# Order of the work between attention and MLP in a one-layer encoder kernel: operand blocks regrouped, residual rows emitted a row later, bias masks stored later

## The chip, the cores and the metric

The kernel runs on one core of a Trainium2 chip. The metric is the device time of one execution in microseconds; each version is run several times and the median counts. Engines are named as in the profile: PE (TensorE, the matrix engine), PEld (its weight loads), DVE (VectorE), ACT (ScalarE), POOL (GpSimd), SP (SyncE, which issues most DMAs; its queue appears as SPq).

## The reference

One layer of an encoder on 2048 tokens of 1024 features, in float32. Two kinds of attention share one input projection and one output projection; a squared-ReLU MLP follows. Each half has its own RMS norm, with shift, scale and gate from a conditioning vector.

```
mod = silu(c) @ w_ada + b_ada            # sh1, sc1, gt1, sh2, sc2, gt2
h = rmsnorm(x, g1) * (1 + sc1) + sh1
q_sb, k_sb, v_sb, q_ca, k_ca, v_ca = split(h @ w_in)
o_sb = stick_breaking_attention(q_sb, k_sb, v_sb)               # 8 heads
o_ca = chunked_relpos_attention(rms(q_ca), rms(k_ca), v_ca, rel_bias)   # 8 heads
x = x + gt1 * (concat(o_sb, o_ca) @ w_o)
h = rmsnorm(x, g2) * (1 + sc2) + sh2
x = x + gt2 * (relu(h @ w1) ** 2 @ w2)
```

## The kernel before, in words

The work is transposed: features lie on the 128 partitions and 512 tokens form a block `tb` (four of them, also numbered `g`). A float32 operand of PE is kept as a high and a low part (type float32r): ACT casts the high part, DVE subtracts it from the value and so makes the low part, and `mm3` multiplies in three matmuls, high by high, high by low and low by high. Eight such triples, 24 matmuls of 128x512, make one output tile (a row) of a projection; a row is here a tile of 128 features by 512 tokens.

The stages in order of time, from the trace:

- 0 to 440 us: the input projection. The queue `behind` carries small jobs that are run some half jobs later than they are put in. `prepare_wo` splits a slice of the output projection's weights (`wo` into `woh` and `wol`) and stores it to `scr_wo`; `prepare_bias` loads a head's bias window `b`, lets POOL write the mask value into two corners, and stores it to `scr_b`. In both, what follows the load is put in with `behind.add(2, rest)`.
- 440 to 1385: both attentions, with other work mixed in as fillers.
- 1385 to 1474: the turn. PE runs the last rows of the output projection. Four rows `po` of token block 1 come from a filler; `row()` advances that filler to its next row. Then eight `Mixed` rows `pso` of token block 0, as the first eight steps of a list `steps`; three of them find their weights in memory (`resident`, tiles `ow`), and five load `wo` tiles of 1 MB from `scr_wo`. In `Mixed.run` the row's `then()` issues the load of the row three further on, and `residual` follows: DVE multiplies the row by its gate and adds it to the old x (tile `xr`, or `cxr` for a `Mixed` row), and SP stores it to `scr_x`. While PE works on the rows, `right_blocks(1, k, ...)` builds the MLP's first operands for token blocks 2 and 3, in four blocks k = 0 to 3: `load` brings four tiles `cy` from `scr_x`, `scale` multiplies each on POOL by the norm and on ACT by the scale with shift, and seven times `put` makes an operand `h{i}_{k}`, for four of them after a difference of two tiles on DVE.
- 1474 to 1760: `First`, seven products for each pair of hidden slices in the manner of Strassen (`ps<-h,opw`; the weights `w` come in pairs, POOL makes their sums `ts`, and ACT and DVE split them into `opw`; `cu`, `cv` and others hold partial results).
- 1760 to about 2100: `Second` for the same half (`ps<-oph,opv`), and in it the second turn: `norm2`, and `right_blocks(0, k, temp)` for token blocks 0 and 1, each of whose nine jobs is hung on a step with `at(n, job)`. Then `First` and `Second` for that half, up to 2714.

No scheduler orders anything: the wrapper `Ordered` keeps each engine's instructions in the order in which the Python code emits them, and SP issues its DMAs in that order too. So an instruction that waits holds everything behind it on its engine. `later.add(n, job)` runs a job n ticks later, and each step ends with one tick. `kept` takes a tile from a pool of 12 buffers (names beginning with c in the trace, like `cy`, `cxr`, `cu`), `temp` one from a pool of 7 (names beginning with t, like `ty`, `ts`). Eight DMAs of SP may be on their way at a time; the ninth waits for the first.

The order of the turn before is written out at the end of the function, as calls of `row()`, `some(k, ...)` (jobs of block k by their number: 0 load, 1 scale, 2 to 8 the seven puts) and `at`.

Of the kernel before, what the change touches and what calls it, by code (L numbers as in the profile page):

```python
# [9 lines left out]
F32 = mybir.dt.float32  # L10
F32R = mybir.dt.float32r
BF16 = mybir.dt.bfloat16
AF = mybir.ActivationFunctionType
ALU = mybir.AluOpType
# [4 lines left out]
P = 128  # L19
# [6 lines left out]
TB = 512  # L26
# [53 lines left out]
def encoder_kernel(ctx, tc, xT, c, g1, g2, w_in, gqk, bias, w_o, w1, w2, w_ada, b_ada, out):  # L80
    nc = tc.nc
    act, dve, pool, sp = nc.scalar, nc.vector, nc.gpsimd, nc.sync
# [61 lines left out]
    later = Later()  # L144

    def split(hi, lo, src, lo_eng=None):
        act.copy(hi, src)
        (lo_eng or dve).tensor_tensor(lo, src, hi.bitcast(F32), op=ALU.subtract)
# [53 lines left out]
    def mm3(ps, st_hi, st_lo, mv_hi, mv_lo, first, last, more=False):  # L202

        pe.matmul(ps, st_hi, mv_hi, start=first, stop=False, skip_group_check=more)
        pe.matmul(ps, st_hi, mv_lo, start=False, stop=False, skip_group_check=more)
        pe.matmul(ps, st_lo, mv_hi, start=False, stop=last, skip_group_check=more)
# [21 lines left out]
    def residual(g, n, ps, xr):  # L228
        dve.scalar_tensor_tensor(xr, ps, mod[:, 2 * KT + n : 2 * KT + n + 1], xr, op0=ALU.mult, op1=ALU.add)
        stores[0].dma_start(scr_x[g, n], xr)  # L230
# [11 lines left out]
    if True:  # L242
# [20 lines left out]
        behind = Later()  # L263
# [117 lines left out]
        def prepare_bias(h):  # L381
            b = stp.tile([P, WIN], F32, tag="bg", name=f"b{h}", bufs=2)
            sp.dma_start(b, bias[h])

            def rest():
                pool.memset(b[0:HD, WIN - HD :], NEG)
                pool.memset(b[HD:P, 0:HD], NEG)
                sp.dma_start(scr_b[h,], b)

            behind.add(2, rest)  # L390

        xts, hts, ws = {}, {}, {}

# [36 lines left out]
        act, dve, pool = (Ordered(tc, e) for e in (act, dve, pool))  # L430
# [75 lines left out]
        act, dve, pool = nc.scalar, nc.vector, nc.gpsimd  # L506
# [21 lines left out]
        for i in range(NH):  # L528
            todo.insert(6 * i + 2, (1.8, lambda i=i: prepare_bias(i)))
            todo.insert(6 * i + 5, (4.4, lambda i=i: prepare_wo(i)))  # L530
# [62 lines left out]
    if True:  # L593
# [391 lines left out]
        rest = 0  # L985
# [24 lines left out]
        def force(f):  # L1010

            got = next(f.gen, None)
            if callable(got):
                got()
            return None if got is None else callable(got)
# [25 lines left out]
        op = ph.enter_context(tc.tile_pool(name="op", bufs=2))  # L1041
# [54 lines left out]
    HK = KT // 2  # L1096
# [5 lines left out]
    if True:  # L1102
# [4 lines left out]
        hop = {k: pm.enter_context(tc.tile_pool(name=f"hop{k}", bufs=1, side="right")) for k in range(2)}  # L1107
# [3 lines left out]
        def operand(src, nm, eng=None, dst=None):  # L1111

            o = opp.tile([P, 2, TB], F32R, tag="op", name=f"op{nm}") if dst is None else dst
            split(o[:, 0, :], o[:, 1, :], src, eng)
            return o
# [8 lines left out]
        def column_sum(eng, out, a, b, op):  # L1124
            eng.tensor_tensor(out, a, b, op=op)
            return out
# [7 lines left out]
        def bank(nm):  # L1134
            return pp.tile([P, TB], F32, tag="ps", name=f"ps{nm}")
# [3 lines left out]
        def at(n, job):  # L1139
            jobs.setdefault(n, []).append(job)  # L1140


        hops = {}
# [33 lines left out]
        def right_blocks(mb, k, home):  # L1177

            y = {}
            tiles = [(nm, 2 * mb + tb, k + HK * kk) for nm, tb, kk in (("11", 1, 0), ("12", 0, 0), ("21", 1, 1), ("22", 0, 1))]  # L1180

            def load():
                for nm, tb, kk in tiles:
                    y[nm] = home(f"y{mb}_{k}_{nm}")
                    sp.dma_start(y[nm], scr_x[tb, kk])

            def scale():
                for nm, tb, kk in tiles:
                    pool.tensor_tensor(y[nm], y[nm], rows[tb], op=ALU.mult)
                    act.activation(  # L1190
                        y[nm], y[nm], AF.Identity, scale=aff[:, 1, kk : kk + 1], bias=mod[:, 3 * KT + kk : 3 * KT + kk + 1]
                    )

            def put(i, nm, a=None, b=None):

                if a:
                    column_sum(dve, y[nm], y[a], y[b], ALU.subtract)
                hops[i, k] = hop[k].tile([P, 2, TB], F32R, tag=f"h{i}_{k}", name=f"h{mb}_{i}_{k}")
                operand(y[nm], "", dst=hops[i, k])

            puts = ((1, "11"), (5, "11", "12", "11"), (3, "22"), (7, "12", "22", "12"))
            puts += ((6, "22", "22", "11"), (2, "21"), (4, "21", "21", "22"))
            return [load, scale] + [lambda x=x: put(*x) for x in puts]


        class Step:
# [5 lines left out]
            def run(self):  # L1212
                pass
# [100 lines left out]
        def second_sums(j, step):  # L1314

            t = []

            def load():
                t.append(raw_pair([P, 2, 2, TB], F32, f"w2s_{j}"))
                for s in range(2):  # L1320
                    sp.dma_start(t[0][:, s].rearrange("p r n -> p (r n)"), w2[2 * j + s])

            def out(i, dst, a, b, op):
                tile = {nm: t[0][:, s, r, :] for nm, s, r in (("11", 0, 0), ("21", 0, 1), ("12", 1, 0), ("22", 1, 1))}
                column_sum(dve, tile[dst], tile[a], tile[b], op)
                sp.dma_start(scr_s[i - 1 if i < 7 else 0, j // 2][:, j % 2, :], tile[dst])

            at(step - (6 if j else 0), load)
            sums = ((5, "22", "21", "22", ALU.add), (7, "21", "11", "21", ALU.subtract))
            sums += ((6, "11", "22", "11", ALU.subtract), (3, "12", "12", "11", ALU.subtract))  # L1330
            for n, x in enumerate(sums):
                at(step + n + (0 if j else 4), lambda x=x: out(*x))
# [81 lines left out]
        class Mixed(Step):  # L1414
# [26 lines left out]
            def run(self):  # L1441
                g, n = self.g, self.n
                w = self.w
                ps = bank(f"o{g}_{n}")
                for k in range(KT):
                    m = Mixed.parts[k]
                    mm3(ps, w[:, 0, k, :], w[:, 1, k, :], m[:, 0, :], m[:, 1, :], k == 0, k == KT - 1)

                self.then()
                residual(g, n, ps, self.xr)  # L1450


        LEFT = 3
# [5 lines left out]
        for mb in (1, 0):  # L1459
            begin = len(steps)  # L1460
            steps += [First(mb, j, i) for j in range(NP) for i in PRODUCTS]
            for j in range(NP):
                f = steps[begin + 7 * j]
                if mb:
                    second_sums(j, begin + 7 * j + 2)
                if j > mb:
                    at(begin + max(7 * j - 13, 2 if mb else -6), f.load)
                    at(begin + 7 * j - 9, f.fetch)
            if not mb:
                at(begin - 8, steps[begin].load)  # L1470
            if mb:
                end = len(steps)
                norm2(1, end - 8)
                norm2(0, end)
                for k in range(HK):
                    begins = end + 16 + 10 * k
                    for n, job in zip((0, 4, 5, 6, 7, 8, 9, 10, 11), right_blocks(0, k, temp)):
                        at(begins + n, job)
            steps += [Second(mb, i, j) for i in PRODUCTS for j in range(NP)]
            for n in range(begin + 7 * NP, len(steps), 2):  # L1480
                at(n - 7, steps[n].load)


        blocks = [right_blocks(1, k, kept) for k in range(HK)]

        def some(k, *ns):
            for n in ns:
                blocks[k][n]()

        left = filler.pop(0)  # L1490

        def row():
            while force(left) is False:
                pass

        steps[0].fetch(0, KT - 2)
        some(0, 0)
        row()
        row()
        some(0, 1, 2, 3, 4)  # L1500
        row()
        some(1, 0)
        some(0, 5, 6, 7, 8)
        steps[0].fetch(KT - 2, KT)
        row()
        some(1, 1, 2, 3, 4)
        row()
        some(2, 0)
        some(1, 5, 6, 7, 8)
        while force(left) is not None:  # L1510
            pass
        hx.close()
# [2 lines left out]
            del resident[n]  # L1515
        for m in range(LEFT):
            steps[m].load()
        for n, (k, *ns) in enumerate(((2, 1, 2, 3, 4), (2, 5, 6, 7, 8), (3, 1, 2, 3, 4), (3, 5, 6, 7, 8))):
            at(n, lambda k=k, ns=ns: some(k, *ns))
        at(0, lambda: some(3, 0))  # L1520
        ready, used = KT, 0
        ahead = iter(steps[1:])
        nxt = next(ahead)
# [57 lines left out]
```

## Time and profile before

| what | before |
| --- | --- |
| runs | 2721.05, 2716.10, 2713.18 us |
| median | 2716.1 us |
| profiled execution | 2715.61 us, its span 2713.8 us |
| mean granted clock of PE | 0.990 |
| busy share of the span | PE 97%, PEld 82%, DVE 69%, ACT 56%, POOL 39% |
| DMA | 650 MB moved, 240 GB/s on average |

The span runs from the first to the last instruction of the core. A row of the timeline gives the start, the length, the engine, the line, the operation, the tile written and the tiles read, a count of instructions in a row, and in brackets the idle time before them with what ended it. Tiles go by names without their numbers. Nearly all instructions have line 42, as the wrapper records them there, so groups are told apart by tiles. A row of a window gives its bounds and length, the busy time of PE, PEld, DVE, ACT and POOL with the number of instructions, the granted clock, the share of the DMA engines and GB/s. A row of the waits view gives who waits for whose tile: the total, the count and the longest.

### The profile page before, as it was taken

What the parts mean: (1) busy time and instruction counts of PE and PEld (TensorE: products, weight loads), DVE (VectorE), ACT (ScalarE), POOL (GpSimd) and SP (SyncE); (2) the same over time, 40 slices, a digit from 0 to 9 for tenths busy, and PEclk for the clock granted to TensorE, in tenths of its full rate; (3) what the DMA queues carried; (4) which work ended last, traced back from release to release, by engine and by line L of the source; (5) the groups of instructions that cost most, each with busy time, mean ns of one, the idle gap of its engine ahead of it and who ended that gap; (6) DMA issues with size and microseconds to landing.
All of it is one profiled execution on the core that took longest, in us unless ns stands there. A gap on an engine that the chain in (4) does not pass through costs nothing. (4 is left out here: it accounts for less than half of the span.)

```text
span 2713.8 us, 42707 instructions
## 1 busy us (share of the span) xinstructions
PE 2622.7 (97%) x14192; PEld 2233.5 (82%) x14192; DVE 1885.1 (69%) x3159; ACT 1518.2 (56%) x2926; POOL 1063.4 (39%) x1296
## 2 busy tenths in 40 slices
PE   6999999899999999999998999999999999999999
PEld 5899998778878987778876888878788888888887
DVE  6435555788789878989755777768866565655565
ACT  5423444788688878878643454455644454444443
POOL 5464265576467656767533333202001323200000
PEclk9999999999999999999998999999999999999999
DMA  9869977978888687756766776795675444465574
GB/s 344 314 247 346 355 290 215 270 248 260 264 258 245 210 259 251 231 186 214 213 228 242 244 270 251 265 334 202 233 259 177 157 144 160 151 233 194 202 264 155
DMA packets 265579, 650.36 MB, mean 240 GB/s; under 512 B 29200, under 2 KB 65040, under 8 KB 255632
## 3 DMA queue, kind: packets, MB, share of 16 engines
q1 hardware_dynamic: 264576, 645.55, 69.7%
q10 hardware_dynamic: 784, 2.10, 0.3%
q8 instruction: 112, 1.84, 0.3%
q14 instruction: 107, 0.88, 0.1%
HBM read 456.16 MB, written 191.37 MB: 239 GB/s over the span
## 5 line engine op out<-in xcount | busy, mean ns | idle before, releaser
L42 PE MATMUL ps<-oph,opv 128*128 128x512 f32 x2688 | 613.6, 390 | 4.7 <-ACT opv L42 2.7
L42 PE MATMUL ps<-h,opw 128*128 128x512 f32 x2664 | 606.4, 390 | 3.7 <-ACT cu L42 3.2
L42 PEld LDWEIGHTS ps<-oph,opv 128*128 128x128 f32 x2688 | 504.0, 188 | 112.4 <-ACT opv L42 4.0
L42 PEld LDWEIGHTS ps<-h,opw 128*128 128x128 f32 x2664 | 501.1, 188 | 108.7 <-ACT cu L42 3.6
L42 POOL TENSOR_TENSOR b<-b,p 128x512 f32<-128x512 f32 (+1 forms) x320 | 360.2, 1126 | 189.0 <-DVE p L42 166.6
L42 DVE TENSOR_TENSOR wtl<-wt,wth 128x512 fp32r<-128x512 f32 (+3 forms) x544 | 290.5, 545 | 49.6 <-ACT wth L42 47.0
L42 ACT CAST wth<-wt 128x512 fp32r<-128x512 f32 (+3 forms) x544 | 257.8, 485 | 115.2 <-PE wt L42 99.3
L42 PE MATMUL pt<-wh,ht 128*128 128x256 f32 x1664 | 305.7, 285 | 0.9 <-DVE qh L42 0.9
L42 DVE TENSOR_TENSOR oph<-hw,oph 128x512 fp32r<-128x512 f32 x224 | 159.9, 714 | 207.1 <-ACT oph L42 206.9
L42 ACT CAST oph<-hw 128x512 fp32r<-128x512 f32 x224 | 139.2, 622 | 277.4 <-PE ps L42 259.3
L42 DVE TENSOR_TENSOR_SCAN p<-z,p,zero 128x512 f32<-128x512 f32 x192 | 246.0, 1281 | 33.2 <-ACT z L42 28.5
L42 PEld LDWEIGHTS pt<-wh,ht 128*128 128x128 f32 x1664 | 262.0, 193 | 1.2 <-ACT st L42 1.1
L42 POOL TENSOR_TENSOR ts<-w 128x512 f32<-128x512 f32 x32 | 44.5, 1392 | 554.6 <-DMA w<-in_w_dram 511.7
L42 PE MATMUL pt<-wl,ht 128*128 128x256 f32 x832 | 236.3, 284 | 3.0 <-POOL wl L42 3.0
L42 PE MATMUL acc<-wth,v 128*128 128x512 f32 (+3 forms) x544 | 222.6, 413 | 0.5 <-DMA v<-scr_v 0.5
L42 ACT ACTIVATE b<-z 128x512 f32<-128x512 f32 (+1 forms) x320 | 171.7, 537 | 64.9 <-PE z L42 47.2
L42 POOL TENSOR_TENSOR e<-e,cols 128x640 f32<-128x640 f32 (+4 forms) x128 | 143.2, 1122 | 144.3 <-DVE cols L42 82.4
L42 PE MATMUL z<-k,q 128*128 128x512 f32 (+3 forms) x640 | 186.5, 373 | 9.7 <-DVE p L42 7.2
L42 PE MATMUL acc<-wtl,v 128*128 128x512 f32 (+3 forms) x544 | 187.0, 350 | 0.0
L42 PE MATMUL wt<-ident,b 128*128 128x128 f32 x1088 | 172.9, 274 | 6.8 <-DVE cols L42 5.1
L42 DVE TENSOR_TENSOR opw<-w,opw 128x512 fp32r<-128x512 f32 x127 | 97.6, 770 | 115.7 <-ACT opw L42 115.5
L42 PE MATMUL po<-fx,ow 128*128 128x512 f32 x576 | 165.9, 403 | 6.2 <-DMA ow<-scr_wo 6.2
(222 smaller groups left out, 4704.8 us busy)
## 6 DMA issues: line engine op xcount, KB each, us to landing
hw<-scr_hid SPq DMA_DIRECT2D x112, 512.0 KB, 3.8
v<-scr_v SPq DMA_DIRECT2D x136, 256.0 KB, 4.3
k<-scr_k SPq DMA_DIRECT2D x268, 128.0 KB, 4.1
w<-in_w_dram SPq DMA_DIRECT2D x64, 512.0 KB, 5.3
hw<-scr_s SPq DMA_DIRECT2D x64, 512.0 KB, 4.6
q<-scr_q SPq DMA_DIRECT2D x124, 256.0 KB, 5.2
fw<-scr_w SPq DMA_DIRECT2D x28, 1024.0 KB, 7.0
wa<-in_w_ada_dram SPq DMA_DIRECT2D x48, 512.0 KB, 7.4
```

The costliest lines, as they stand in the source:

```text
L42: return lambda *x, **y: self.tc.keep_in_program_order(f(*x, **y))
```

## The change

1. `prepare_bias` masks and stores four half jobs after the load instead of two.
2. The seven puts of a block are taken apart into `high` (ACT's cast), `low` (DVE's subtraction) and `less` (a difference), and put together again in three groups `plain`, `mixed` and `rest`, in which parts and differences alternate, so that several casts stand between a cast and its own subtraction. A block has five jobs instead of nine, and in the second turn they are hung on steps 0, 4, 6, 8 and 10.
3. Block 0 of the first turn takes its four tiles from `temp` instead of `kept`.
4. A `Mixed` row's residual is put in with `later.add(2, ...)`: it is emitted a row later.
5. In the turn, one more `row()` stands ahead of block 0's load, `row()` advances the filler by one step more, past that row's own residual, and the jobs of the blocks are spread over the rows anew.

The instructions of each engine are the same in kind and number, and PE's order is the same; on ACT, DVE, POOL and SP only the order changes.

```
-            behind.add(2, rest)
+            behind.add(4, rest)
...
-            def put(i, nm, a=None, b=None):
-
-                if a:
-                    column_sum(dve, y[nm], y[a], y[b], ALU.subtract)
+            def high(i, nm):
                 hops[i, k] = hop[k].tile([P, 2, TB], F32R, tag=f"h{i}_{k}", name=f"h{mb}_{i}_{k}")
-                operand(y[nm], "", dst=hops[i, k])
-
-            puts = ((1, "11"), (5, "11", "12", "11"), (3, "22"), (7, "12", "22", "12"))
-            puts += ((6, "22", "22", "11"), (2, "21"), (4, "21", "21", "22"))
-            return [load, scale] + [lambda x=x: put(*x) for x in puts]
+                act.copy(hops[i, k][:, 0, :], y[nm])
+
+            def low(i, nm):
+                dve.tensor_tensor(hops[i, k][:, 1, :], y[nm], hops[i, k][:, 0, :].bitcast(F32), op=ALU.subtract)
+
+            def less(nm, a, b):
+                column_sum(dve, y[nm], y[a], y[b], ALU.subtract)
+
+            def plain():
+                high(1, "11")
+                high(3, "22")
+                low(1, "11")
+                high(2, "21")
+                low(3, "22")
+                less("11", "12", "11")
+
+            def mixed():
+                high(5, "11")
+                low(2, "21")
+                less("12", "22", "12")
+                high(7, "12")
+                low(5, "11")
+                less("22", "22", "11")
+
+            def rest():
+                high(6, "22")
+                low(7, "12")
+                less("21", "21", "22")
+                high(4, "21")
+                low(6, "22")
+                low(4, "21")
+
+            return load, scale, plain, mixed, rest
...
                 self.then()
-                residual(g, n, ps, self.xr)
+                later.add(2, lambda: residual(g, n, ps, self.xr))
...
-                    for n, job in zip((0, 4, 5, 6, 7, 8, 9, 10, 11), right_blocks(0, k, temp)):
+                    for n, job in zip((0, 4, 6, 8, 10), right_blocks(0, k, temp)):
                         at(begins + n, job)
...
-        blocks = [right_blocks(1, k, kept) for k in range(HK)]
+        blocks = [right_blocks(1, k, kept if k else temp) for k in range(HK)]
...
         def row():
             while force(left) is False:
                 pass
+            return force(left)
 
         steps[0].fetch(0, KT - 2)
+        row()
         some(0, 0)
         row()
-        row()
-        some(0, 1, 2, 3, 4)
+        some(0, 1)
         row()
         some(1, 0)
-        some(0, 5, 6, 7, 8)
+        some(0, 2, 3, 4)
         steps[0].fetch(KT - 2, KT)
         row()
-        some(1, 1, 2, 3, 4)
+        some(1, 1, 2)
+        some(2, 0)
         row()
-        some(2, 0)
-        some(1, 5, 6, 7, 8)
+        some(1, 3, 4)
         while force(left) is not None:
             pass
...
-        for n, (k, *ns) in enumerate(((2, 1, 2, 3, 4), (2, 5, 6, 7, 8), (3, 1, 2, 3, 4), (3, 5, 6, 7, 8))):
+        for n, k, *ns in ((0, 2, 1, 2), (1, 2, 3, 4), (1, 3, 0), (3, 3, 1, 2), (4, 3, 3, 4)):
             at(n, lambda k=k, ns=ns: some(k, *ns))
-        at(0, lambda: some(3, 0))
```

By the emitted order, SP now has the last `ow` load ahead of block 0's four loads; the first `wo` load ahead of block 3's four loads; the second `wo` load ahead of the store of the first `Mixed` row (row 5 of the output), behind which it stood before, and the third behind that store. On DVE the residual of row 5 now stands behind all of block 2; those of the later rows stand inside or behind block 3, and the last behind the first operands of the second weight pair. In the input projection's stage the later stores of `b` stand behind the next loads of `wo`.

## The prediction, made before the run

> **What bounds the kernel now.** I begin with the page's busy times and then cut the span at the stage borders.
>
> ```profile
> PE 2622.7 (97%) x14192; PEld 2233.5 (82%) x14192; DVE 1885.1 (69%) x3159; ACT 1518.2 (56%) x2926; POOL 1063.4 (39%) x1296
> 1385.00:1474.00 89.00, 74.04 (x294) 58.85 (x293) 43.74 (x57) 30.05 (x47) 26.52 (x19) 0.90 0.72 251
> 1474.00:1760.00 286.00, 282.84 (x1241) 233.65 (x1241) 220.67 (x297) 134.99 (x239) 96.26 (x63) 0.99 0.72 256
> 1820.00:1945.00 125.00, 121.86 (x537) 99.06 (x536) 99.88 (x136) 73.18 (x131) 27.03 (x21) 1.00 0.63 221
> ```
>
> TensorE is the bound of the whole: 97% busy. The columns behind the window are its length, then busy time of PE, PEld, DVE, ACT and POOL, and then the granted clock. The turn (1385 to 1474) stands out: PE is busy for 74.04 of 89 us, at a clock of 0.90. The change leaves TensorE's instructions and their order as they are, so it can only move PE's idle time and its slow clock. The timeline of PE shows both.
>
> ```profile
> 1385.39 11.14 PE L42 MATMUL po<-fx,ow 128*128 128x512 f32 x48
> 1402.74 13.28 PE L42 MATMUL po<-fx,ow 128*128 128x512 f32 x48 [6.21 <-DMA ow<-scr_wo]
> 1415.86 16.48 PE L42 MATMUL pso<-opm,ow 128*128 128x512 f32 x72
> 1435.62 8.39 PE L42 MATMUL pso<-opm,wo 128*128 128x512 f32 x24 [3.28 <-DMA wo<-scr_wo]
> 1447.42 7.32 PE L42 MATMUL pso<-opm,wo 128*128 128x512 f32 x24 [3.41 <-DMA wo<-scr_wo]
> 1455.29 5.74 PE L42 MATMUL pso<-opm,wo 128*128 128x512 f32 x24 [0.54 <-DMA wo<-scr_wo]
> 1461.51 5.72 PE L42 MATMUL pso<-opm,wo 128*128 128x512 f32 x24 [0.48 <-DMA wo<-scr_wo]
> 1468.27 5.71 PE L42 MATMUL pso<-opm,wo 128*128 128x512 f32 x24 [1.03 <-DMA wo<-scr_wo]
> 1473.81 5.60 PE L42 MATMUL ps<-h,opr 128*128 128x512 f32 x24
> 1488.01 12.34 PE L42 MATMUL ps<-h,opw 128*128 128x512 f32 x46 [3.16 <-ACT cu L42]
> ...
> 1400.00:1405.00 5.00, 2.26 (x5) 1.82 (x6) 2.62 (x5) 2.46 (x4) 0.22 (x1) 0.54 0.95 346
> 1435.00:1440.00 5.00, 4.38 (x10) 3.47 (x11) 4.29 (x5) 1.14 (x2) 2.56 (x2) 0.50 0.00 0
> 1445.00:1450.00 5.00, 2.58 (x8) 2.09 (x9) 2.64 (x4) 3.65 (x6) 0.00 (x0) 0.82 0.57 156
> ```
>
> A row of 24 matmuls takes 5.60 us undisturbed. Waits: 6.21 for `ow`, then 3.28, 3.41, 0.54, 0.48 and 1.03 for the five `wo`, and 3.16 for `cu`: 18.1 us. Behind each long wait the clock halves: 48 matmuls take 13.28 instead of 11.14 (2.1 us more), and rows take 8.39 and 7.32 instead of 5.60 (2.8 and 1.7); about as much again (estimate 1.7) behind `cu`. Together 26 us is what there is to win in the turn.
>
> Who makes the weights late? SP's timeline and the waits of the turn say it.
>
> ```profile
> 1385.58 9.49 SPq L42 DMA_DIRECT2D cy<-scr_x  x4
> 1395.59 0.43 SPq L42 DMA_DIRECT2D ow<-scr_wo  x1
> 1414.45 7.57 SPq L42 DMA_DIRECT2D scr_x<-xr  x2
> 1427.59 0.48 SPq L42 DMA_DIRECT2D wo<-scr_wo  x1
> 1440.29 0.41 SPq L42 DMA_DIRECT2D wo<-scr_wo  x1
> 1447.61 0.41 SPq L42 DMA_DIRECT2D wo<-scr_wo  x1
> 1462.46 1.52 SPq L42 DMA_DIRECT2D w<-in_w_dram  x2
> 1478.21 0.90 SPq L42 DMA_DIRECT2D w<-in_w_dram  x2
> ...
> SPq L42 <- DVE cxr L42: 30.0, 5, 11.3
> SPq L42 <- DMA scr_m<-os: 7.9, 1, 7.9
> DVE h L42 <- ACT h L42: 25.3, 19, 9.8
> ```
>
> SP issues in program order, and a store of a residual row stands ahead of each weight load. From issue to PE's start a weight tile takes 7.15 us (1395.59 to 1402.74), 8.0 (1427.59 to 1435.62), 7.1 (1440.29 to 1447.42) and 7.7 (1447.61 to 1455.29). So SP's queue, held 30.0 us by VectorE's `cxr`, sets the turn; VectorE in turn waits 19 times for ScalarE's half of `h`.
>
> **The turn, step by step.** Block 0's four loads now go to temporary tiles and stand behind the last `ow`, where the 9.49 us stood ahead of it. But 7.9 of those 9.49 were not theirs: a slot was held by the store `scr_m`, which is issued elsewhere and keeps its place. The `ow` load inherits this wait, and goes out at about 1393.8 (1385.58 plus 7.9 and a little) instead of 1395.59. With the 7.15 us it would be there at 1401.0; with 1 MB less ahead of it in the transfers at the 346 GB/s of the window shown (3.0 us) at 1398. I take 1399.8, in the middle: a wait of 3.3 instead of 6.21, and 1.7 us of slow clock instead of 2.1. Gain 3.3 (2 to 5.5).
>
> The five rows up to 1432.34 then end at about 1429.0. The first `wo` stood behind block 3's four loads and two stores that waited for block 1 on VectorE (7.57). Now it is ahead of the block's loads, and the last `xr` residual comes inside block 1 rather than behind half of it; I put its issue at 1424.0 (estimate: 1.8 us of loads gone, the rest from the faster block), and with 7 to 8 us it is there at 1431 to 1432. Wait about 2, slow clock 1, where 6.1 stood: this row ends at about 1437.5 instead of 1444.0. Its successor's `wo` stays ahead of the store of row 5 now (it was behind it, at 1440.29), held only by a tile of block 3 that comes free at block 1's end: issue at about 1431, there at 1438.5. Wait 1, clock 0.5; that row ends at about 1444.6 instead of 1454.7: ten us ahead.
>
> There the change gives back. The third `wo` stands behind the store of row 5, and this row's residual is now a row later: in VectorE's order it stands behind all of block 2.
>
> ```profile
> 1424.94 2.26 DVE L42 TENSOR_TENSOR h<-cy,h 128x512 fp32r<-128x512 f32 x2 [0.69 <-ACT h L42]
> 1433.13 1.62 DVE L42 TENSOR_TENSOR h<-cy,h 128x512 fp32r<-128x512 f32 x1 [2.54 <-ACT h L42]
> 1445.34 0.69 DVE L42 TENSOR_TENSOR h<-cy,h 128x512 fp32r<-128x512 f32 x1 [0.68 <-ACT h L42]
> ```
>
> Block 2 takes VectorE from 1433.13 to 1446.03. It has seven lower parts and four differences, 11 operations; at 0.69 that is 7.6 us, and the interleaving takes away most of the waits of 0.69 for ScalarE (four in a block: 2.8). Some of the operations take 1.62 while POOL multiplies. Started at 1433.5 (POOL has then finished block 1's and most of block 2's products), it ends between 1441.5 and 1446; I take 1443.5. The residual (0.75), the store's issue (0.4) and the `wo` behind it: issue at 1444.8, there at 1452 (7.1). So PE waits about 7 us in front of the third row, a wait that was 0.54, and pays 2 us of clock. The row starts at 1452 instead of 1455.29. The last two `wo` find their residuals earlier in block 3 and wait for nothing: 1452 plus three rows of 5.6 and the 2 us ends at 1470.8 against 1473.81, gain 3.0 (0 to 6).
>
> Behind it, `cu`:
>
> ```profile
> 1483.68 1.28 POOL L42 TENSOR_TENSOR ts<-w 128x512 f32<-128x512 f32 x1 [6.08 <-DMA w<-in_w_dram]
> ```
>
> The copy `cu` stands on ScalarE behind casts of the second weight pair, issued at 1478.21 behind the last two stores and summed by POOL from 1483.68. The pair's load is now ahead of the last row's store, and the first pair's casts, for which its issue at 1462.46 waited, come earlier. I take the wait at 1.5 instead of 3.16 and the clock at 0.8 instead of 1.7: gain 2.5 (−1 to 4.9). The turn: 5.5.
>
> **The second turn.** Blocks of the first half are built between 1835 and 1945 under PE's products.
>
> ```profile
> PE ps L42 <- DVE oph L42: 1.3, 1, 1.3
> PE ps L42 <- ACT opv L42: 1.2, 2, 0.8
> ```
>
> PE waits 2.5 us there for operands that queue behind block work. With parts grouped and differences between them, VectorE and ScalarE no longer wait for one another there. But a group is now five or six operations at once, about 2 us on either engine, and can itself hold an operand. I take a gain of 2.0 (−1.5 to 2.8); no group is longer than a row.
>
> **The bias.** Only masking and storing move, two half jobs later.
>
> ```profile
> 310.19 1.18 SPq L42 DMA_DIRECT2D wo<-in_w_o_dram  x1
> 318.75 1.05 ACT L42 CAST woh<-wo 128x1024 fp32r<-128x1024 f32 x1 [4.45 <-DMA wo<-in_w_o_dram]
> 326.84 0.39 PE L42 MATMUL pt<-wl,ht 128*128 128x256 f32 x1 [2.32 <-POOL wl L42]
> 328.53 0.51 PE L42 MATMUL pt<-wl,ht 128*128 128x256 f32 x1 [0.71 <-POOL wl L42]
> ...
> 325.00:328.50 3.50, 0.97 (x6) 0.77 (x6) 2.89 (x3) 0.00 (x0) 3.30 (x5) 1.00 0.91 313
> 328.60:332.00 3.40, 3.40 (x16) 3.40 (x17) 0.53 (x2) 1.99 (x2) 0.93 (x1) 0.50 1.03 387
> ```
>
> PE loses 3.0 us in waits for `wl` and 1.7 us at a clock of 0.50. The cause lies on ScalarE: its cast of `woh` waits for a load that SP issued at 310.19, just behind a bias store, and the casts for `wl` stand behind it. With the store behind the load, the load goes out about 0.5 us earlier and shares the way with less. I take 1.0 of waiting and half a us of clock: 1.5 (0 to 4.7). Masks and stores elsewhere lie under PE's work; a mask held longer keeps one of two staging tiles for two half jobs more, and the next load into that tile is six half jobs away, so nothing waits.
>
> **A rule weighed.** At 325.00 to 328.50 PE was idle in pieces of 2.32 and 0.71 us only, and the clock halved for the 3.4 us that followed. The Trainium skill (TensorE: Matmul & The Clock Gate, "What's actually happening" and "Why this matters for your kernels") says that the array falls to half its clock after an idle window of about 3.4 us, and advises against gaps of over about 3 us; by that, short waits cost nothing but themselves. The trace disagrees: the gaps here are shorter. It would make a rival, below.
>
> **The sum.** 5.5 + 2.0 + 1.5 = 9.0 us. The profiled execution took 2715.61 (span 2713.8 and 1.8 around it); the median of the runs, 2716.1, is 0.5 above. That gives 2706.6 by the profiled execution and 2707 for a median. A measurement of this kernel tells about 0.3% (8.1 us) from no change, so the band of no change is 2708 to 2724, and my number lies at its edge.
>
> **Rivals.** (a) Block 2 is not late. If the block ends by 1438, the third `wo` is there at 1446.5, the new wait shrinks to 2 us and most of its slow clock goes: 5.5 and 1.5 us more, 2700. For it: 7.6 us of operations are all that it must take; against: POOL's multiplies, four of some 1.3 us, stand ahead of it. Chance 0.18. (b) Short waits cost no clock: all waits of mine below 3 us (2, 1, 1.5 and the one at 326.84) lose their shares of clock, 1 + 0.5 + 0.8 + 1.2 = 3.5 us: 2703.5. Against it stand the two windows at 325 and 328.6. Chance 0.07. This is what the skill's rule above would give. (c) No change: the new wait for the third `wo` takes all that was won ahead of it. That is so from a block 2 that ends on VectorE at 1446.5, half a us behind today's end, since 1446.5 + 1.3 + 7.1 + 18.8 = 1473.7; what is left is `cu`, the second turn and the bias, 0 to 6 us: about 2712. For it: the residual is the only thing that moved back, and two others may be worth nothing. Chance 0.30. (d) Slower: VectorE becomes the bound of the rows. If POOL's multiplies overlap all of both blocks, an operation takes 1.62 and not 0.69, block 2 needs 17.8 us and ends at 1451.3, block 3 the same; the third `wo` arrives at 1460 and the fifth, behind a residual in the middle of block 3, at 1469, so that the rows end at 1476 to 1480 with slow clock, the casts for `cu` slip as far, and VectorE comes to the second weight pair 8 us late: 10 to 14 us lost against 0 to 3 won, 2725. It decides from a block 2 that ends behind 1454 or both blocks at over 1.4 us an operation. Against it: POOL works 5.2 us for a block, which covers three operations of eleven. Chance 0.08. (e) The `ow` load keeps its time, because the slot's wait goes with it entirely: then the first step gives 1.8 of its 3.3 us, but the new wait in front of the third row takes up the difference, as its start hangs on VectorE; the time is the forecast's to within 1 us. It has no chance of its own.
>
> **How the numbers follow.** The forecast has 0.37, at 2702 to 2712 by its own bounds; about 0.27 of it lies under 2708 and 0.10 above. Faster by over 0.3%: 0.27 + 0.18 + 0.07 = 0.52, and 0.02 of (c), at its best: 0.54. Slower by over 0.3%: 0.06 of (d), as its lower half stays in the band. Within: 0.10 + 0.28 + 0.02 = 0.40. The range leaves out (d) at the top and the tails of (a) with every step at its best: 2696 to 2719.
>
> **What would show it.** Right: a wait of 2.5 to 4.5 us in front of the `po` row at 1400; the first `wo` issued at 1423 to 1426; a new wait of 5 us or more in front of the third `wo` row, with SP held by `cxr` just before; `ps<-h,opr` from 1469 to 1472; DVE's waits for ScalarE's `h` at half of their 25.3 us or less; no wait over 1 us between 1835 and 1945. The forecast is wrong if the third `wo` row starts behind 1455 or ahead of 1448, if PE waits anew between 1475 and 1530, or if the attention stage, in which nothing moves, shifts by more than 3 us.

## The result and the profile after

| | before | after |
| --- | --- | --- |
| median of 7 runs | 2717.44 us (2713.18 to 2721.05) | 2709.25 us (2705.25 to 2711.81) |
| ratio, 95% interval | | 0.9969 (0.9956 to 0.9981) |
| profiled execution, its span | 2715.61, 2713.8 | 2706.24, 2704.4 |

The kernel is 0.31% faster, which is 8.4 us by the ratio (the medians are 8.2 us apart); the forecast was 9 us. The page's line of busy times is nearly unchanged, as PE does the same work in less idle time. The timeline of PE in the turn, of the changed kernel:

```profile
PE 2616.3 (97%) x14192; PEld 2231.1 (82%) x14192; DVE 1885.4 (70%) x3159; ACT 1516.7 (56%) x2926; POOL 1065.6 (39%) x1296
...
1383.49 11.14 PE L42 MATMUL po<-fx,ow 128*128 128x512 f32 x48
1397.21 7.33 PE L42 MATMUL po<-fx,ow 128*128 128x512 f32 x24 [2.59 <-DMA ow<-scr_wo]
1404.96 5.69 PE L42 MATMUL po<-fx,ow 128*128 128x512 f32 x24 [0.42 <-DMA ow<-scr_wo]
1410.49 16.48 PE L42 MATMUL pso<-opm,ow 128*128 128x512 f32 x72
1431.03 13.21 PE L42 MATMUL pso<-opm,wo 128*128 128x512 f32 x48 [4.05 <-DMA wo<-scr_wo]
1452.54 18.12 PE L42 MATMUL pso<-opm,wo 128*128 128x512 f32 x72 [8.30 <-DMA wo<-scr_wo]
1470.50 5.60 PE L42 MATMUL ps<-h,opr 128*128 128x512 f32 x24
1475.94 30.11 PE L42 MATMUL ps<-h,opw 128*128 128x512 f32 x132
1507.49 22.87 PE L42 MATMUL ps<-h,opw 128*128 128x512 f32 x98 [1.44 <-DVE cx L42]
```

Five waits of the old turn are shorter or gone (`ow`, the second `wo`, the last two `wo`, `cu`). The first `wo` is waited for 0.8 us longer (4.05), the third `wo` has a new wait of 8.30 us, and `cx` one of 1.44. SP's timeline and the waits of the turn show why:

```profile
1392.15 0.32 SPq L42 DMA_DIRECT2D ow<-scr_wo  x1
1395.66 0.41 SPq L42 DMA_DIRECT2D ow<-scr_wo  x1
1424.37 0.40 SPq L42 DMA_DIRECT2D wo<-scr_wo  x1
1431.32 0.38 SPq L42 DMA_DIRECT2D wo<-scr_wo  x1
1444.44 0.32 SPq L42 DMA_DIRECT2D scr_x<-cxr  x1
1445.33 0.40 SPq L42 DMA_DIRECT2D wo<-scr_wo  x1
1471.47 0.90 SPq L42 DMA_DIRECT2D w<-in_w_dram  x2
...
SPq L42 <- DVE cxr L42: 18.2, 3, 12.7
SPq L42 <- DMA scr_m<-os: 6.0, 1, 6.0
DVE h L42 <- ACT h L42: 12.5, 4, 6.5
...
1434.30 2.76 DVE L42 TENSOR_TENSOR h<-cy,h 128x512 fp32r<-128x512 f32 x2 [2.65 <-ACT h L42]
1442.29 1.46 DVE L42 TENSOR_TENSOR h<-cy,h 128x512 fp32r<-128x512 f32 x2
1443.67 1.41 DVE L42 SCALAR_TENSOR_TENSOR cxr<-pso,mod,cxr 128x512 f32<-128x512 f32 x2
```

The store of row 5 (1444.44) waited 12.7 us for its residual, which VectorE ran at 1443.67, just behind block 2's last part; the third `wo` went out behind the store and one load of 256 KB. VectorE's waits for ScalarE's `h` fell from 19 to 4. One thing stated ahead of the prediction does not hold: the last `ow` load (1395.66) still stands behind block 0's loads; it is the last but one (1392.15) that now goes out ahead of them.

The second turn has no wait of PE left. The four rows with a wait and the window of the kernel before, then the window of the changed one:

```profile
1894.72 2.60 PE L42 MATMUL ps<-oph,opv 128*128 128x512 f32 x10 [0.34 <-DVE opv L42]
1898.10 27.94 PE L42 MATMUL ps<-oph,opv 128*128 128x512 f32 x120 [0.78 <-ACT opv L42]
1926.47 6.40 PE L42 MATMUL ps<-oph,opv 128*128 128x512 f32 x25 [0.43 <-ACT opv L42]
1934.14 16.08 PE L42 MATMUL ps<-oph,opv 128*128 128x512 f32 x68 [1.27 <-DVE oph L42]
1835.00:1945.00 110.00, 106.86 (x463) 86.38 (x462) 90.92 (x123) 65.21 (x116) 23.87 (x15) 1.00 0.62 220
...
1831.00:1937.00 106.00, 106.00 (x469) 87.81 (x468) 91.93 (x125) 66.82 (x118) 24.94 (x15) 1.00 0.67 233
```

PE's matmuls have the same order in all kernels here, so the start of the same matmul can be compared. The table cuts the trace at fixed matmuls (numbers of PE's instruction in parentheses); lengths in us. "Turn" runs from the `po` row to the matmul that starts at 1514.2 in the kernel before, the "1514-us mark" of the expectations.

| kernel | first stage (34 to 3080) | attention (to 8496) | turn (to 8940) | rest of First (to 10200) | second turn (to 10800) |
| --- | --- | --- | --- | --- | --- |
| before | 412.6 | 943.7 | 128.8 | 288.7 | 137.9 |
| before_again | 411.0 | 944.1 | 130.2 | 291.7 | 136.1 |
| bias4_only | 409.9 | 945.9 | 128.9 | 287.9 | 136.8 |
| second_turn_only | 414.1 | 945.9 | 131.1 | 288.4 | 133.1 |
| after | 408.0 | 945.9 | 124.0 | 291.4 | 132.5 |
| after_again | 416.0 | 946.9 | 126.1 | 289.7 | 132.8 |
| after_bias2 | 410.6 | 943.7 | 126.9 | 289.7 | 132.5 |
| after_kept0 | 408.4 | 945.0 | 126.4 | 291.3 | 132.9 |
| after_pingpong | 408.5 | 944.9 | 130.0 | 292.9 | 133.0 |
| after_resid_now | 408.0 | 938.2 | 124.4 | 288.4 | 132.6 |
| resid_now_again | 410.7 | 943.3 | 123.0 | 289.6 | 133.0 |
| resid_now_w2_early | 410.2 | 945.2 | 123.0 | 289.1 | 133.0 |
| after_block2_late | 408.4 | 945.3 | 124.5 | 291.2 | 132.6 |
| late_w2_early | 410.5 | 942.5 | 120.7 | 290.7 | 133.0 |

From matmul 10800 to the last one it is 768.6 us in every kernel. With nothing changed the first column moves by up to 8 us (after and after_again: 408.0 and 416.0) and the second by up to 5 (after_resid_now and resid_now_again: 938.2 and 943.3). Among kernels with the same turn, that column moves by 2 to 3 us; the second turn moves by under 2. So single profiles are compared below only with this spread in mind: the profile `after` has the shortest turn of the four that have it alike (after, after_again, after_bias2, after_kept0).

### The profile page after: what moved, and what is told of

It reads as the page before. It is cut to its first block, busy times and chain, and to the rows that moved or that the text cites. A ratio compares the mean times of both kernels' runs of the same rounds, so it can differ in the third digit from the quotient of the medians.

```text
span 2704.4 us, 42721 instructions
## 1 busy us (share of the span) xinstructions
PE 2616.3 (97%) x14192; PEld 2231.1 (82%) x14192; DVE 1885.4 (70%) x3159; ACT 1516.7 (56%) x2926; POOL 1065.6 (39%) x1296
## 5 line engine op out<-in xcount | busy, mean ns | idle before, releaser
L42 DVE TENSOR_TENSOR wtl<-wt,wth 128x512 fp32r<-128x512 f32 (+3 forms) x544 | 290.5, 545 | 51.3 <-ACT wth L42 49.1
L42 ACT ACTIVATE z<-z 128x512 f32<-128x512 f32 (+1 forms) x320 | 170.6, 533 | 0.0
```

What stands on the lines that cost most here:

```text
L42: return lambda *x, **y: self.tc.keep_in_program_order(f(*x, **y))
```

## The experiments

**before_again: the kernel before, profiled a second time.** No edit.

> The kernel before, profiled a second time, as a measure of how far the same program's stages move from one execution to another. Theory (the attention stage is paced by its loads, so that PE's waits there depend on when it arrives): the waits of the turn (6.2, 3.3, 3.4 us) and the one of 3.0 us near 325 us come again to within 0.5 us, and the start of the turn's po row, 1385.4, comes again to within 1 us. Rival (the 2.8 us that the changed kernel lost between 440 and 1385 are chance): that start moves by 2 us or more with nothing changed.

2719.1 us. The timeline of PE near 325 us and at the turn:

```profile
328.67 0.39 PE L42 MATMUL pt<-wl,ht 128*128 128x256 f32 x1 [0.43 <-POOL wl L42]
...
1386.24 11.14 PE L42 MATMUL po<-fx,ow 128*128 128x512 f32 x48
1403.58 13.29 PE L42 MATMUL po<-fx,ow 128*128 128x512 f32 x48 [6.21 <-DMA ow<-scr_wo]
1470.83 5.70 PE L42 MATMUL pso<-opm,wo 128*128 128x512 f32 x24 [2.21 <-DMA wo<-scr_wo]
```

The turn's large waits came again (6.21 to the hundredth, the first two `wo` to 0.4), its start within 0.9 us; those for the last two `wo` were 1.64 and 2.21 instead of 0.48 and 1.03. The wait near 325 did not: 0.43 instead of 2.32, with 0.70 behind it, and no slow clock. So that wait is not a property of the kernel, and the two profiles alone cannot say what the bias edit does.

**bias4_only: the bias edit alone, in the kernel before.**

```
-            behind.add(2, rest)        # prepare_bias
+            behind.add(4, rest)
```

> The kernel before with the bias masks and stores two half jobs later, and nothing else. Theory: the waits at 326.8 and 328.5 (2.3 and 0.7 us) and the half clock behind them go, PE is 4.7 us ahead at 440 us, and attention takes 2 to 3 of them back in waits for its loads of k and fw, so that the turn starts 1.9 us earlier and the whole gains about 2 us (2714). Rival (the loss in attention is chance, or comes of the turn's edits): all 4.7 us stay, about 2711.

2714.78 us, ratio 0.9990 (0.9976 to 1.0003). PE does not wait near 326 us, and the lead of 2.2 us that it has at the first stage's end is gone by the turn, which starts at 1385.4 as before. The time is the theory's, but the interval holds no change as well; that attention takes a lead back as such cannot be told from its own spread. The table's first stage points to about 2 us: 409.9 on average in the ten profiles with the edit (408.0 to 416.0), 412.1 in the four without it (410.6 to 414.1); but the ranges overlap.

**after_bias2: the changed kernel without the bias edit.**

```
-            behind.add(4, rest)        # prepare_bias
+            behind.add(2, rest)
```

> The changed kernel with the bias masks and stores back at two half jobs. Theory: the waits at 326 us are back, the turn starts at 1385 to 1386, the rest as in the changed kernel: a span of about 2706.5, a gain of 7 to 8 us on the kernel before, of which the turn with cu has 5.7 and the second turn 4. Rival (the parts are not independent; a later arrival at the turn changes its waits): the turn from its po row to the second product takes over 1 us more or less than the 97.9 us of the changed kernel.

2710.61 us, ratio 0.9967 (0.9952 to 0.9981), as with the edit. PE did not wait near 326 us, although the masks were early, while after_again (the changed kernel, profiled a second time) waited there with the masks late. These rows are of after_again:

```profile
331.67 0.39 PE L42 MATMUL pt<-wl,ht 128*128 128x256 f32 x1 [1.76 <-POOL wl L42]
...
1394.11 11.14 PE L42 MATMUL po<-fx,ow 128*128 128x512 f32 x48
```

The expected return of the waits failed. The rival's sign came, the second product 100.5 us behind the turn's start instead of 97.9; but after_again has 100.8 with the bias edit in place, so this too is spread. By bias4_only's interval the edit is worth between 0.8 us of loss and 6.5 us of gain, and between after and after_bias2 no difference shows.

**after_again: the changed kernel, profiled and timed a second time.** No edit. Expected was a turn of 124.0 us again to within 1 us, and an attention stage anywhere between 938.2 and 945.9 us if its length is chance, or within 1 us of 945.9 if each kernel has its own.

2709.45 us, ratio 0.9969 (0.9956 to 0.9981), as the first time. The turn took 126.1 us, 2.1 more, so the first of these failed; attention took 946.9, outside the first range and just within 1 us of 945.9, though the next two profiles (938.2 and 943.3 for one kernel) speak against a fixed length too; the first stage was 8.0 us longer. Rows of VectorE (the residual of row 5 behind block 2) and PE:

```profile
1456.01 1.40 DVE L42 SCALAR_TENSOR_TENSOR cxr<-pso,mod,cxr 128x512 f32<-128x512 f32 x2
...
1464.74 19.40 PE L42 MATMUL pso<-opm,wo 128*128 128x512 f32 x72 [8.51 <-DMA wo<-scr_wo]
1483.98 5.60 PE L42 MATMUL ps<-h,opr 128*128 128x512 f32 x24
```

The turn's start is 1394.11 here. Counted from it, the residual ran at 61.9 us and the products started at 89.9; in the first profile these were 60.2 and 87.0.

**after_resid_now and resid_now_again: the residual in its own step.**

```
-                later.add(2, lambda: residual(g, n, ps, self.xr))
+                residual(g, n, ps, self.xr)
```

> The changed kernel with the residual of a Mixed row emitted in its own step again instead of a row later. Theory (the residual behind all of block 2 makes the third wo late): the wait of 8.3 us in front of the third wo row falls under 2 us, but the second wo now stands behind the store of row 5, and its row waits 5 to 8 us instead of 0.15; the products start within 1.5 us of the changed kernel's 1470.5. Rival (the third wo is late for another reason, such as its buffer coming free late): the wait in front of the third row stays at 6 us or more and the second row's stays short.

> The changed kernel with the residual of a Mixed row in its own step, unaltered from the earlier run, beside the changed kernel on the same chip. Theory (its turn is as long as the changed kernel's, 124.4 against 124.0 us, so the rest of its lead was chance): its median comes out within 3 us of the changed kernel's. Rival (its lead is its own): it stays ahead by 5 us or more, with attention again near 938 us.

2703.21 us, ratio 0.9937 (0.9917 to 0.9956), then 2703.82, ratio 0.9953 (0.9940 to 0.9966), against 2709.45 of after_again beside the second (0.9969, 0.9956 to 0.9981). Timelines of PE and SP, first run:

```profile
1425.47 7.05 PE L42 MATMUL pso<-opm,wo 128*128 128x512 f32 x24 [5.22 <-DMA wo<-scr_wo]
1440.21 24.45 PE L42 MATMUL pso<-opm,wo 128*128 128x512 f32 x96 [7.68 <-DMA wo<-scr_wo]
1464.50 5.60 PE L42 MATMUL ps<-h,opr 128*128 128x512 f32 x24
...
1430.13 0.33 SPq L42 DMA_DIRECT2D scr_x<-cxr  x1
1432.95 0.38 SPq L42 DMA_DIRECT2D wo<-scr_wo  x1
```

As the theory said, the third row's wait is gone and the second row waits 7.68 us, because its `wo` stands behind the store of row 5 again. The new wait changed its row; its size stayed. The products started 88.7 us behind the turn's start, 1.7 later than in the profile `after`, a little outside the 1.5 expected, and 87.5 the second time. But the lead of 5.6 us came again, where the theory of chance allowed 3, and attention was not near 938 the second time, so the rival's reason falls too. By the table the three kernels with the residual in its own step spend 123.5 us in the turn on average and 289.0 from there to the second turn; the four that are the changed kernel in both respects, or differ from it in bias or buffers, 125.9 and 290.5. In that stretch PE waited 0.7 to 1.7 us for `cx` in those four, and not in these. That is 3.9 of the 5.6 us; the rest stays open. By these runs the edit to emit the residual a row later is a loss of some 5 us in the median.

**after_block2_late: the late residual, but ahead of two thirds of block 2.**

```
-        ... (0, 2, 1, 2), (1, 2, 3, 4), (1, 3, 0), (3, 3, 1, 2), (4, 3, 3, 4)
+        ... (0, 2, 1, 2), (1, 3, 0), (2, 2, 3, 4), (3, 3, 1, 2), (4, 3, 3, 4)
```

> The changed kernel with the second and third group of block 2's parts one step later, so that on VectorE the residual of row 5 stands ahead of them, while the second wo stays ahead of that row's store. Theory (the third wo is late because this residual waits for block 2's end at 1443.7): the residual runs at about 1438, the third wo goes out at about 1440 and its row waits under 3 us instead of 8.3; the second row's wait stays near 0; the products start 4 to 6 us earlier in the turn than in the changed kernel. Rival (the late parts of block 2 and block 3 then hold the fourth and fifth wo or the first products): a new wait of 3 us or more in front of the fourth or fifth wo row or of the first product, and the gain falls under 2 us.

2706.22 us, ratio 0.9964 (0.9951 to 0.9977). Timelines of PE, VectorE and SP:

```profile
1439.55 5.72 PE L42 MATMUL pso<-opm,wo 128*128 128x512 f32 x24 [0.79 <-DMA wo<-scr_wo]
1447.07 7.39 PE L42 MATMUL pso<-opm,wo 128*128 128x512 f32 x24 [1.79 <-DMA wo<-scr_wo]
1481.27 40.03 PE L42 MATMUL ps<-h,opw 128*128 128x512 f32 x168 [3.28 <-ACT cu L42]
...
1439.22 0.74 DVE L42 SCALAR_TENSOR_TENSOR cxr<-pso,mod,cxr 128x512 f32<-128x512 f32 x1
...
1470.62 0.98 SPq L42 DMA_DIRECT2D scr_x<-cxr  x2
1471.70 0.90 SPq L42 DMA_DIRECT2D w<-in_w_dram  x2
```

The theory of the third `wo` holds: the residual ran at 1439.22 and the wait fell from 8.30 to 1.79. The products started 82.7 us behind the turn's start instead of 87.0 (89.1 on average over the four profiles with the changed kernel's turn). Most of the gain was given back at once, though not where the rival had it: `cu` waits 3.28 us, and the turn as a whole takes 124.5, against 124.0 in the profile `after` and 125.9 on average. The median is 3 us lower than the changed kernel's. SP shows the next bound: the second weight pair goes out at 1471.70, as in the changed kernel (1471.47), behind the stores of rows 2 and 3. In the changed kernel this load was just early enough, because the rows were late.

**late_w2_early: and the second weight pair's load ahead of those stores.**

```
-                steps[n + LEFT].load() if n + LEFT < KT else steps[KT].fetch() if n + LEFT == KT else None
+                steps[n + LEFT].load() if n + LEFT < KT else steps[KT].fetch() if n + LEFT == KT
+                else steps[KT + 7].load() if n == KT - 2 else None
```

> The kernel with block 2's second and third group a step later, and in addition the load of the second weight pair issued behind row 2's weights instead of behind the stores of rows 2 and 3. Theory (cu is late because that pair's load stands behind a residual that VectorE runs only behind the first weight pair's parts, at 1469.9): the load goes out near 1461 instead of 1471.7, the wait of 3.3 us for cu and its slow clock go, and the turn ends 4 to 5 us earlier than without this edit; with the 4.3 us that the rows had won the kernel is about 4 us ahead of the changed one. Rival (cu waits for the first weight pair and for POOL's sums): the wait for cu stays at 2 us or more.

2704.40 us, ratio 0.9945 (0.9931 to 0.9958). The timelines of PE and SP:

```profile
1447.45 18.13 PE L42 MATMUL pso<-opm,wo 128*128 128x512 f32 x72 [3.76 <-DMA wo<-scr_wo]
1470.86 30.39 PE L42 MATMUL ps<-h,opw 128*128 128x512 f32 x132
...
1460.17 0.87 SPq L42 DMA_DIRECT2D w<-in_w_dram  x2
```

The load went out 11.5 us earlier, the wait for `cu` is gone, and the turn fell from 124.5 to 120.7 us, the shortest of all. The median is 5 us under the changed kernel's (2709.25 and 2709.45); the intervals of the two ratios overlap only between 0.9956 and 0.9958. It is no faster than the kernels with the residual in its own step (2703.2 and 2703.8), although its turn is shorter.

**resid_now_w2_early: the same load in the kernel with the residual in its own step.** The edit as above.

> The changed kernel with the residual in its own step, and the second weight pair's load issued behind row 2's weights. Theory as before: PE does not wait for cu here (0.04 us), so the early load can win little: within 2 us of the same kernel without it, about 2703. Rival (the early load lets the first products' later operands come earlier too): 3 us or more better, with less waiting on PE between 1465 and 1530.

2704.52 us, ratio 0.9944 (0.9931 to 0.9956); 2703.82 without it. The turn is 123.0 both ways: where `cu` isn't waited for, the early load wins nothing.

**second_turn_only: the regrouped blocks in the second turn alone.**

```
-            return [load, scale] + [lambda x=x: put(*x) for x in puts]
+            if mb == 0:
+                return [load, scale, plain, mixed, rest]
+            return [load, scale] + [lambda x=x: put(*x) for x in puts]
...
-                    for n, job in zip((0, 4, 5, 6, 7, 8, 9, 10, 11), right_blocks(0, k, temp)):
+                    for n, job in zip((0, 4, 6, 8, 10), right_blocks(0, k, temp)):
```

> The kernel before with the regrouped parts and differences in the second turn alone, the first turn and the bias as before. Theory (casts and subtractions that no longer wait for one another let the operands of the products through): no wait over 0.3 us between 1820 and 1945, where there were 0.34, 0.78, 0.43 and 1.27, so 2.5 to 4 us of that stretch go and the rest stays: about 2713 to 2714. Rival (the second turn gains because the first turn left other engines further ahead): the waits stay, and the time is that of before.

2711.85 us, ratio 0.9981 (0.9971 to 0.9991): 5.2 us, 2.4 to 7.9. The second turn takes 133.1 us instead of 136.1 to 137.9, with no wait over 0.3 us. The part stands by itself and does not need the first turn's edits.

**after_pingpong: the same jobs at the same steps, each low part right behind its high part.**

```
+            def part(i, nm):
+                high(i, nm)
+                low(i, nm)
+
             def plain():
-                high(1, "11")
-                high(3, "22")
-                low(1, "11")
-                high(2, "21")
-                low(3, "22")
+                part(1, "11")
+                part(3, "22")
+                part(2, "21")
                 less("11", "12", "11")
...              # mixed and rest likewise
```

> The changed kernel with the same jobs at the same steps, but inside each job a low part directly behind its high part on VectorE, so that ScalarE's casts keep their order and VectorE waits for each of them as before the change. Theory (the interleaving of parts and differences ends the second turn's waits): VectorE's waits for ScalarE's h come back (over 15 us between 1380 and 1475, 12.5 in the changed kernel), the second turn, 132.5 us in the changed kernel from PE's 1799 to 1931, takes 1.5 us or more longer, the first turn 1 us. Rival (the steps on which the jobs are hung do it): the second turn stays within 0.5 us of 132.5 and the time with the changed kernel's.

2714.09 us, ratio 0.9979 (0.9970 to 0.9988). Timeline and waits of the turn, and the second turn's only wait:

```profile
1433.53 13.54 PE L42 MATMUL pso<-opm,wo 128*128 128x512 f32 x48 [7.33 <-DMA wo<-scr_wo]
1457.95 18.77 PE L42 MATMUL pso<-opm,wo 128*128 128x512 f32 x72 [10.88 <-DMA wo<-scr_wo]
...
DVE h L42 <- ACT h L42: 15.6, 17, 2.6
...
1897.52 52.66 PE L42 MATMUL ps<-oph,opv 128*128 128x512 f32 x231 [0.17 <-DVE opv L42]
```

The result splits the theory. The first turn loses all that it had won: 130.0 us, as before the change, since VectorE waits 17 times again and both the first and the third `wo`, whose loads stand behind residuals in VectorE's order, are waited for 3.3 and 2.6 us longer than in the profile `after`. The second turn stays at 133.0, although 4.8 of the 8.9 us that VectorE waited there for ScalarE's `h` in the kernel before are back. So there it isn't the interleaving of casts and their own subtractions: the three groups on every other step are enough.

**after_kept0: block 0 in the larger pool again.**

```
-        blocks = [right_blocks(1, k, kept if k else temp) for k in range(HK)]
+        blocks = [right_blocks(1, k, kept) for k in range(HK)]
```

> The changed kernel with block 0 of the first turn in the pool of 12 buffers again instead of the temporary one. Theory (with 12 buffers, blocks 0 to 2 fill them together with the residual rows, so that the loads of block 2 or 3 wait for a tile): SP waits 2 us or more longer for a tile of a block (3.3 us for cy in the changed kernel), and the second or third wo goes out later by as much. Rival (the buffers are no limit): SP's waits for cy stay within 1 us of 3.3 and the rows start as in the changed kernel, 47.5 and 69 us behind the turn's start.

2708.24 us, one run. SP's wait for a tile of a block is 2.1 us, not longer, and the rows behind `wo` start 50.0 and 71.1 us behind the turn's start, as in after_again (49.4 and 70.6). The rival's own marks (a wait within 1 us of 3.3, rows at 47.5 and 69) came from the profile `after` and were missed, by 0.2 us for the wait and 2.1 to 2.5 us for the rows; but after_again, whose pool is not altered, is 1.6 to 1.9 us behind them as well. The pool is no limit here, and the theory fails.

## Why the prediction was right, step by step

The time came out as forecast, but not as the sum of the steps forecast. The step that was to win 3.0 us up to the products won nothing on average, and what stands behind it won more than was put down.

- **The `ow` load.** 3.3 us of waiting predicted, 2.59 and 0.42 measured; the load was held 6.0 us by the store `scr_m`, whose wait it took over, and went out at 1392.15. PE reached it 13.7 us behind the turn's start instead of 17.4: 3.6 us, and 3.3 were predicted.
- **The first and second `wo`.** Issues predicted at 1424.0 and 1431, measured 1424.37 and 1431.32. That these times agree so well is partly luck: the turn had started 1.9 us earlier, so counted from its start both loads came some 2.2 us later than predicted, and 2.4 to 4.4 us in the three other profiles with this turn. As PE came earlier, it waited 4.05 us instead of 2 for the first, and 0.15 instead of 1 for the second.
- **The third `wo`,** the step that carried the forecast. The prediction found the place where the change gives back: the load stands behind row 5's store, which stands behind block 2 on VectorE, and after_block2_late showed this cause. Its wait was put at 7 us and measured 8.30. The time was too early. Block 2's end was predicted 58.1 us behind the turn's start (1443.5); it came at 60.2 in the first profile and at 61.9, 61.7 and 62.5 in after_again, after_bias2 and after_kept0. VectorE began block 2's parts at 50.8 to 51.8, not at 48.1; their length, put at 10 us, was 9.4 to 10.7. In the first profile alone, by the time at which the residual ran (1443.67), the step looks right to a fifth of a microsecond.
- **The products.** A gain of 3.0 was predicted. Between the profiles `before` and `after` it is 1.4 (87.0 us behind the turn's start against 88.4). In the four profiles with the new turn the products start at 87.0, 89.9, 89.6 and 89.9, in the four with the old one at 88.4, 90.1, 88.6 and 89.4: on average the gain is nothing. The new wait takes all that was won ahead of it. This is what rival (c) had, from a block 2 that ends at 1446.5, which is 61.1 us behind the turn's start; only what is left behind the products was more than the 0 to 6 us that it allowed.
- **`cu`.** 2.5 us predicted, for the reason that the runs show: the load of the second weight pair goes out earlier (88.0 us behind the turn's start instead of 92.8), and late_w2_early shows that this load decides the wait. The wait and its slow clock are gone, but PE waits anew for `cx`, 0.7 to 1.7 us in the four profiles; a new wait of PE between 1475 and 1530 was one of the prediction's own signs of being wrong, and it came (1.44 us at 1507.49). The whole turn: 5.5 predicted, 4.8 in the two profiles, 3.9 as the mean of four kernels with the old turn (129.8) and four with the new one (125.9), all of it behind the products' start.
- **The second turn.** 2.0 predicted, 4.2 measured (136.9 as the mean of three, 132.7 of four). The size was off, because the waits cost more than their idle time: in the profile before, PE lost 5.3 us against the changed kernel over four waits of 2.8 us in sum, at a granted clock of 1.00; what the rest is, no run shows. The reason was off as well: the prediction put it down to engines that wait for one another, and after_pingpong showed the groups and their steps to be enough. The interleaving is what the first turn needs.
- **The bias.** 1.5 predicted. The first stage seems to show it (412.6 us in `before`, 408.0 in `after`), but before_again, after_bias2 and after_again showed the wait to come and go with either order. What the edit is worth stays open between −0.8 and 6.5 us.
- **Attention.** The prediction said that a shift of over 3 us there would speak against it. It shifted by 2.2 us in the two profiles and by up to 8.7 us between others (938.2 to 946.9) whose order there is the same: such a bound on one profile tests nothing.

The sum of turn and second turn by the means is 8.1 us, against 8.4 measured. Between them, the rest of First is 1.3 us longer on average in the four with the new turn (290.5 against 289.2), within its spread. The forecast of 9.0 came near because its errors cancelled: the turn 1.6 too much, the second turn 2.2 too little, and 1.5 for the bias, which no run shows.

## What to carry to other kernels

Where loads and stores share one in-order queue, follow each load back to the store ahead of it, and that store to the instruction it waits for, on its own engine's order: the change put a wait of 8 us in front of another row, at the place that the order foretold; its time, counted from the turn's start, came 2 to 4 us later than was worked out from rows. When a wait is taken away, look for the next load behind the same kind of store; here removing the wait for the third `wo` shortened the turn by 1.4 us against the changed kernel's average, and by 5.2 once the second weight pair's load had been moved too. And profile the unchanged kernel and the changed one twice before reading a small stage difference as an effect, and count rows from the stage's start.

## What the runs showed of the hardware

The clock halved after waits of well under 3.41 us, depending on where they lay. In the traces the granted clock changes only on a fixed grid of steps of 3.41 us. In after_block2_late a wait of 1.79 us lay within one step (1445.0 to 1448.4); the clock was 0.50 in the next, and the row took 7.39 us instead of 5.60. In before_again a wait of 2.21 us lay across two steps, with 1.0 and 1.2 in each; the clock stayed, and the row took 5.70. Over all fourteen traces, behind the first 50 us, no step at full clock with less than 1.4 us of idle PE was followed by a slowed one, and every one with more than 1.9 us was. Between these two, both happened; since the ends of matmuls are modelled, the bounds are rough. The Trainium skill (TensorE: Matmul & The Clock Gate, "What's actually happening") speaks of an idle window of about 3.4 us; the free-running window agrees, but the traces show a shorter idle time to be enough.
